# A gate's block ahead of the step from 32 to 64, and the bonus' sum behind the values

## The chip, the core and the metric

The kernel runs on one core of one Trainium2 chip. Five engines have instruction queues of their own: TensorE (PE, with its weight loads as PEld), VectorE (DVE), ScalarE (ACT), GpSimd (POOL) and SyncE (SP), which here only issues DMAs. The metric is the device time of one execution in microseconds (us).

## The reference: what is computed

One layer of a streaming encoder on 2048 tokens of width 1024, in float32:

```
h   = rms_norm(x)
P   = h @ w_in            # q,k,v of attention | r,k,v,w,a,g of the RWKV-7 branch | gates
yA  = chunk_band_attention(q, k, v)
yB  = rwkv7_time_mix(...)
m   = sigmoid(gA) * (yA @ proj_a) + sigmoid(gB) * (yB @ proj_b)
x   = x + rms_norm(m @ w_out)
x   = x + rms_norm(relu(rms_norm(x) @ w_up)^2 @ w_down)
```

The RWKV branch is, per head of 64 channels, a recurrence over time:

```
sa    = state @ aa_t
state = state * w_t + sa (x) bb_t + v_t (x) k_t
y_t   = state @ r_t
bonus = sum(r_t * k_t * r_k) * v_t
out   = (group_norm(y) + bonus) * g
```

The kernel computes it in chunks of 64 tokens. Within a chunk the recurrence becomes the inverse of a 64x64 unit triangular matrix, and between the chunks only a 64x64 state is carried.

## The kernel before

**Groups.** The first half works on four groups of 512 tokens: for each, `phase_rwkv`, then `phase_attention`, then `phase_merge`. The feed-forward layer follows (`phase_up`, `phase_down`); the change does not touch it.

**Dense blocks.** `dense(col)` multiplies 128 columns of `w_in` with the group's normed activations. Float32 is made of two rounded parts, so a block is 3 x 8 = 24 products of 128x128 by 128x512 (line 75). Its weights are loaded by SyncE (line 60), rounded by ScalarE (`whi`, line 66) and their low half is made by VectorE (`wlo`, line 67); there are two buffers of each, and two result banks (`psd`). The last product is kept as `self.mm`. A gate (`gate(i)`, line 657) is one such block, with a tanh on ScalarE (line 661) and a write to DRAM from ScalarE's queue; a group has 16 of them, and they are needed only in the merge, so that they can stand anywhere in the phase. `mix` (line 284) is such a block with the token shift behind it.

**One RWKV phase.** Eight heads are four pairs of heads, in two batches of two pairs. For each pair `rwkv_pre` makes r, k and v, the decays, the bonus and the chunks' matrices. For a batch `rwkv_inverse` inverts the two diagonal 32x32 blocks of every triangular matrix, with a chain of 31 steps of two instructions each on VectorE (lines 503 and 509), and turns the result into `X1` (line 512). `rwkv_blocks` then takes the step from 32 to 64: 64 small products of `NA` and `X1` on PE (line 533), a copy to `Z` on ScalarE (line 535), 64 small products of `Z` and `XT` (line 540), and a copy into `XT`. `rwkv_trans` makes the chunks' transitions, `recurrence` runs over the eight chunks (lines 613 to 616), and `rwkv_post` normalises the output (`yn`, line 634), transposes it (line 641), adds the bonus and multiplies with `g` (lines 651, 654).

**What sets the order.** The program is traced in one order, in which the generators `rec_of` and `rwkv_inverse` are advanced by hand between other work: `GATES` says how many gates the first `rwkv_pre` draws at its eight `between()` places, `STEPS` how many steps of the first batch's `rec_of` are traced at the places of the second batch's two `rwkv_pre`. Gates are drawn from one iterator, and once its 16 are gone a call of `gate()` does nothing. A planner in the compiler then fills each engine's queue: of the instructions that it reckons ready it takes the one traced first, so that later work can stand ahead of work traced before it which it holds for not ready yet. Once planned, an engine runs its queue in order and waits where an operand is not there.

In the first batch the step is traced at the first `between()` of the third pair, behind its r, k and v blocks. In the second batch it is traced behind the inverse, the first batch's post and one gate:

```
            rec = rec_of(NA, nxt, 1)
            for n in (4, 6, None):
                advance(rec, n)
                gate()
            gate(2)
            post = [self.rwkv_post(2 + q, nxt[q]) for q in range(2)]
```

In `rwkv_pre` the bonus' sum (a product of r*k*r_k with a block of ones, `ps_bonus`, line 426) stands ahead of the centred values' products (`ps_v`, line 435). Both take their banks from a pool with two buffers (`self.pa`), as do the transposes behind them (`ps_bk`, line 450).

Of the kernel before, what the change touches and what calls it, by code (L numbers as in the profile page):

```python
# [8 lines left out]
F32 = mybir.dt.float32  # L9
# [3 lines left out]
ALU = mybir.AluOpType  # L13
# [4 lines left out]
P = 128  # L18
# [5 lines left out]
G = 512  # L24
GT = G // P
C = 64
NC = G // C
# [10 lines left out]
RW0 = 1536  # L38
GATE0 = 1536 + 1792


def advance(steps, n=None):

    while n is None or n > 0:
        if next(steps, steps) is steps:
            return
        n = n and n - 1


class Block:  # L50
    def __init__(self, tc, a, out):
# [284 lines left out]
    def rwkv_pre(self, g, p, rp, NA, between=lambda: None):  # L336
        nc = self.nc
# [3 lines left out]
        r = self.tmp("r")  # L341
# [3 lines left out]
        ps = self.lora(0, p)  # L345
# [5 lines left out]
        ps = self.lora(1, p)  # L351
        ta = self.tmp("ta")
        nc.scalar.activation(ta, ps, AF.Tanh, scale=0.5, bias=self.ha0[:, col])
        v = self.tmp("v")
# [67 lines left out]
        between()  # L422

        nc.vector.scalar_tensor_tensor(r, r, self.rk[:, col], tk, op0=ALU.mult, op1=ALU.mult)
        psb = self.pa.tile([P, G], F32, tag="a", name="ps_bonus")
        nc.tensor.matmul(psb, self.bones, r, start=True, stop=True)
        nc.vector.tensor_tensor(r, psb, v, ALU.mult)
        nc.gpsimd.dma_start(self.bvd[p], r)

        between()  # L430

        SV = rp.tile([P, NC, 2, C], F32, tag="SV", name="SV")
# [4 lines left out]
        for h in range(2):  # L437
            src = psv[h * C : h * C + C]
            nc.scalar.copy(SVv[C:P, h, :, 0], src[:, :, 0:C])
            nc.scalar.copy(SVv[0:C, h, :, 1], src[:, :, C:P])  # L440
        R["SV"] = SV

        between()

# [15 lines left out]
        q = p % 2  # L460
        mS = self.mS[:, None, :].to_broadcast((P, 4, C))
        for h in range(2):
# [3 lines left out]
            for j in range(4):  # L466
                c = h * 4 + j
# [53 lines left out]
            nc.scalar.copy(XT[par * C : par * C + 32, :, :, 0:32], XD[par * C : par * C + 32])  # L521
        self.X1, self.XT = X1, XT

    def rwkv_blocks(self, NA, Rs):

        nc, X1, XT = self.nc, self.X1, self.XT
        Z = self.ip.tile([P, 2, NC, 32], F32, tag="Z", name="Z")
        parts = [(slice(r, r + 32), slice(r + 32, r + C)) for r in (0, C)]
        ps = self.pa.tile([P, 2, NC, 32], F32, tag="a", name="ps_t1")
        for q in range(2):  # L530
            for c in range(NC):
                for lo, hi in parts:
                    nc.tensor.matmul(ps[hi, q, c], NA[lo, q, c, 32:64], X1[lo, q, c], start=True, stop=True)
        for lo, hi in parts:
            nc.scalar.copy(Z[hi], ps[hi])
        ps = self.pa.tile([P, 2, NC, 32], F32, tag="a", name="ps_t2")
        for q in range(2):
            for c in range(NC):
                for lo, hi in parts:
                    nc.tensor.matmul(ps[lo, q, c], Z[hi, q, c], XT[hi, q, c, 32:64], start=True, stop=True)  # L540
        for lo, hi in parts:
            nc.scalar.copy(XT[lo, :, :, 32:64], ps[lo])
        for q in range(2):
            Rs[q]["XT"] = XT[:, q]
# [112 lines left out]
    def gate(self, i):  # L657
        nc = self.nc
        ps = self.dense(GATE0 + i * P)
        t = self.sp.tile([P, G], F32, tag="gate", bufs=2, name="gate")  # L660
        nc.scalar.activation(t, ps, AF.Tanh, scale=0.5, bias=self.hgb[:, i : i + 1])
        nc.scalar.dma_start(self.gd[i // 2][:, i % 2], t)

    def phase_rwkv(self, g):
        tc = self.tc
        with ExitStack() as ctx:
            def pool(name, bufs, **kw):
                return ctx.enter_context(tc.tile_pool(name=name, bufs=bufs, reuse_waits="tile", **kw))

            rp = pool("rw", 3)  # L670
            self.tp = pool("rwt", 9)
            self.ip = pool("rwi", 1)
            self.xp = pool("rwx", 2)
            self.lp = pool("rwl", 1)
            self.sp = pool("rws", 2)
            self.pa = pool("rwpa", 2, space=PSUM)
            self.pr = pool("rwpr", 2, space=PSUM)
            self.py = pool("rwpy", 2, space=PSUM)

            def pairs():  # L680
                return self.ip.tile([P, 2, NC, C], F32, tag="NA", name="NA")

            gates = iter(range(2 * KB))

            def gate(n=1):
                for i in range(n):
                    i = next(gates, None)
                    if i is not None:
                        self.gate(i)

            def places(plan, act):
                it = iter(plan)
                return lambda: act(next(it, 0))

            def rec_of(NA, Rs, b):
                self.rwkv_blocks(NA, Rs)
                yield
                for q in range(2):
                    yield from self.rwkv_trans(2 * b + q, Rs[q])
                    yield  # L700
                yield from self.recurrence(b, Rs)

            self.lora_wa(g)
            NA = pairs()
            between = places(GATES, gate)
            Rs = [self.rwkv_pre(g, q, rp, NA, between) for q in range(2)]
            inv = self.rwkv_inverse(NA, rp)
            for _ in range(2):
                advance(inv, 8)
                gate()  # L710
            advance(inv, 6)
            self.lora_g(g)
            advance(inv)
            gate()
            rec = rec_of(NA, Rs, 0)
            NA = pairs()
            between = places(STEPS, lambda n: advance(rec, n))
            nxt = [self.rwkv_pre(g, 2 + q, rp, NA, between) for q in range(2)]
            inv = self.rwkv_inverse(NA, rp)
            for n in (1, 4):  # L720
                advance(rec, n)
                gate()
            advance(rec)
            post = [self.rwkv_post(q, Rs[q]) for q in range(2)]
            for p in post:
                advance(p, 1)
            for _ in range(3):
                advance(inv, 8)
                gate()
            advance(inv)  # L730
            for p in post:
                advance(p)
# [7 lines that stand above are left out]
            for p in post:  # L740
                advance(p, 1)
            gate(2 * KB)
            for p in post:
                advance(p)
# [505 lines left out]
            self.phase_up(1, zp, rp, cb, pn, 8)  # L1250
            self.phase_down(1, zp, rp, cb, pn, lambda op, pt: iter(()))


_INS = [
    "x", "pre_mix_g", "w_in", "gate_bias", "rel_rev", "shift_mu", "w0", "w2", "a0", "a2", "g2",
    "k_k", "k_a", "r_k", "ln_x_w", "ln_x_b", "proj_a", "proj_b", "w_out", "post_mix_g",
    "pre_ffn_g", "w_up", "w_down", "post_ffn_g",
]


def layout(inputs):
    import numpy as np
# [7 lines left out]
            v = v.reshape(-1)  # L1270
        got[name] = np.ascontiguousarray(v)
    return got


# [15 lines left out]
```

## Time and profile before

| | |
|---|---|
| median of 3 runs | 3447.2 us (3445.45 to 3448.03) |
| profiled execution | 3443.36 us, its span 3441.7 us |
| mean granted clock of TensorE | 0.984 |
| TensorE, idle ahead of `ps_t` (line 533) | 26.6 us, 8 times |
| TensorE, idle ahead of `ps_bonus` (line 426) | 8.1 us, 8 times |

A row of the order of time gives the start and the duration in us, the engine, the line, the operation, what it writes and reads, the shape and the count; in brackets stands how long the engine was idle before it and what ended that. A row of the list of waits gives who waited for whom, the total in us, the number of times and the longest. A row of the table by stretches gives the stretch, its length, each engine's busy time with its count, the granted clock of TensorE (1 is full speed), the DMA share and GB/s. Times count from the start of the span. Products overlap in the array, so a product that lasts 0.39 us can start 0.23 us behind the one before it.

### The profile page before, as it was taken

What the parts mean: (1) busy time and instruction counts of PE and PEld (TensorE: products, weight loads), DVE (VectorE), ACT (ScalarE), POOL (GpSimd) and SP (SyncE); (2) the same over time, 40 slices, a digit from 0 to 9 for tenths busy, and PEclk for the clock granted to TensorE, in tenths of its full rate; (3) what the DMA queues carried; (4) which work ended last, traced back from release to release, by engine and by line L of the source; (5) the groups of instructions that cost most, each with busy time, mean ns of one, the idle gap of its engine ahead of it and who ended that gap; (6) DMA issues with size and microseconds to landing.
All of it is one profiled execution on the core that took longest, in us unless ns stands there. A gap on an engine that the chain in (4) does not pass through costs nothing. (4 is left out here: it accounts for less than half of the span.)

```text
span 3441.7 us, 50336 instructions
## 1 busy us (share of the span) xinstructions
PE 3301.4 (96%) x19233; PEld 2679.8 (78%) x19233; DVE 2414.4 (70%) x4110; ACT 1414.3 (41%) x2319; POOL 411.9 (12%) x796
## 2 busy tenths in 40 slices
PE   7999999999998999998999989999999999999998
PEld 5777777777876777876777877888888878888886
DVE  5774856766856775866774875777887788776667
ACT  4434634436644445644435634333331243331112
POOL 2210002111003110002210000111200021100001
PEclk9999999999999999999999999999999999999999
DMA  5223353125365225355224277434855374343233
GB/s 147 83 87 125 130 200 104 56 87 192 120 218 162 65 93 167 128 204 179 77 87 141 90 243 239 135 117 137 285 169 184 99 241 133 119 144 98 98 98 110
DMA packets 397864, 481.10 MB, mean 140 GB/s; under 512 B 17516, under 2 KB 304432, under 8 KB 397624
## 3 DMA queue, kind: packets, MB, share of 16 engines
q1 hardware_dynamic: 346168, 364.63, 33.2%
q0 software_dynamic: 23040, 79.71, 6.1%
q10 hardware_dynamic: 28416, 33.56, 2.8%
q8 instruction: 151, 2.47, 0.3%
q14 instruction: 89, 0.73, 0.1%
HBM read 356.16 MB, written 124.81 MB: 140 GB/s over the span
## 5 line engine op out<-in xcount | busy, mean ns | idle before, releaser
L75 PE MATMUL ps_dn<-fop 128*128 128x512 f32 x3072 | 700.9, 390 | 3.5 <-DVE u L1170 3.4
L75 PEld LDWEIGHTS ps_dn<-fop 128*128 128x128 f32 x3072 | 575.7, 188 | 125.1 <-DVE u L1170 5.2
L75 PE MATMUL psd<-hh,whi 128*128 128x512 f32 x1344 | 546.4, 407 | 9.7 <-ACT whi L66 8.8
L75 PE MATMUL psd<-hl,whi 128*128 128x512 f32 x1344 | 544.4, 405 | 0.0
L75 PE MATMUL psd<-hh,wlo 128*128 128x512 f32 x1344 | 541.2, 403 | 0.6 <-DVE wlo L67 0.5
L66 ACT CAST whi<-wraw 128x1024 fp32r<-128x1024 f32 x232 | 243.4, 1050 | 514.0 <-PE psd L75 411.1
L1170 DVE TENSOR_TENSOR u<-u,ps_dn 128x512 f32<-128x512 f32 x480 | 323.1, 685 | 148.5 <-PE ps_dn L75 148.0
L67 DVE TENSOR_TENSOR wlo<-wraw,whi 128x1024 fp32r<-128x1024 f32 x232 | 283.0, 1220 | 201.3 <-ACT whi L66 183.2
L75 PEld LDWEIGHTS psd<-hh,whi 128*128 128x128 f32 x1344 | 258.9, 193 | 63.3 <-ACT whi L66 10.0
L75 PEld LDWEIGHTS psd<-hh,wlo 128*128 128x128 f32 x1344 | 258.3, 192 | 51.7 <-DVE wlo L67 2.8
L75 PEld LDWEIGHTS psd<-hl,whi 128*128 128x128 f32 x1344 | 258.6, 192 | 50.3
L66 ACT CAST fop<-wdraw 128x1024 fp32r<-128x1024 f32 x64 | 67.0, 1047 | 424.0 <-DVE u L1170 321.2
L1091 POOL DMA_DIRECT2D ad<-r x128 | 69.5, 543 | 587.0 <-DVE r L1090 570.9
L75 PE MATMUL ps_p<-yh,whi 128*128 128x512 f32 x256 | 102.9, 402 | 10.7 <-DVE th L931 8.6
L66 ACT CAST s12h<-s 128x1024 fp32r<-128x1024 f32 x32 | 33.8, 1055 | 184.6 <-PE ps_u L75 184.6
L823 DVE CUSTOM_DVE_ANT_0 sc<-bias,ps_s 128x640 f32<-128x640 f32 (+4 forms) x128 | 93.5, 730 | 22.1 <-PE ps_pt L835 17.9
L960 PE MATMUL ps_o<-whi,mh 128*128 128x512 f32 x256 | 102.1, 403 | 5.1 <-ACT whi L66 3.5
L828 ACT ACTIVATE sc<-sc,mn 128x640 f32<-128x640 f32 (+4 forms) x128 | 97.7, 763 | 19.3 <-DVE mn L823 18.7
L839 ACT CAST PTh<-ps_pt 128x640 fp32r<-128x640 f32 (+4 forms) x128 | 80.0, 625 | 58.6 <-PE ps_pt L835 56.6
L75 PE MATMUL ps_p<-yh,wlo 128*128 128x512 f32 x256 | 103.0, 403 | 0.1
L75 PE MATMUL ps_p<-yl,whi 128*128 128x512 f32 x256 | 102.9, 402 | 0.0
L840 DVE TENSOR_TENSOR PTl<-ps_pt,PTh 128x640 fp32r<-128x640 f32 (+4 forms) x128 | 94.3, 737 | 12.1 <-ACT PTh L839 11.1
(352 smaller groups left out, 6648.8 us busy)
## 6 DMA issues: line engine op xcount, KB each, us to landing
wraw<-in_w_in_dram SPq DMA_DIRECT2D x168, 512.0 KB
wraw<-in_w_up_dram SPq DMA_DIRECT2D x80, 512.0 KB
ad<-r POOLq DMA_DIRECT2D x128, 256.0 KB, 2.6
wdraw<-in_w_down_dram SPq DMA_DIRECT2D x64, 512.0 KB
araw<-ad SPq DMA_DIRECT2D x64, 512.0 KB
gd<-gate ACTq DMA_DIRECT2D x64, 256.0 KB
th<-gd SPq DMA_DIRECT2D x32, 512.0 KB
wraw<-in_w_out_dram SPq DMA_DIRECT2D x32, 512.0 KB
```

What stands on the lines that cost most here:

```text
L66: self.nc.scalar.copy(hi, src)
L67: self.nc.vector.tensor_tensor(lo, src, hi.bitcast(F32), ALU.subtract)
L75: mm = nc.tensor.matmul(ps, l, r, start=n == 0, stop=n == last).ins
L823: nc.vector.tensor_tensor_reduce(sc[:, 0:n], bias[:, s0:640], pss[:, c0 : c0 + n], 1.0, 3.0e38, ALU.add, ALU.min, mn,)
L828: nc.scalar.activation(sc[:, 0:n], sc[:, 0:n], AF.Exp, scale=-1.0, bias=mn, accum_out=sm)
L839: nc.scalar.copy(hv, pst[:, 0:nk])
L840: nc.vector.tensor_tensor(lv, pst[:, 0:nk], hv.bitcast(F32), ALU.subtract)
L960: nc.tensor.matmul(ps[t], l[:, k, ts], r[:, k % 2], start=k == 0 and j == 0, stop=k == KB - 1 and j == 2)
L1091: nc.gpsimd.dma_start(self.ad[fb][:, th], r)
L1170: nc.vector.tensor_tensor(u[t][:, ns], u[t][:, ns], ps, ALU.add)
```

## The change

Two things. First, `rec_of` draws a gate ahead of the step, in both batches, and the first half of the step (the 64 products of line 533 and the copy to `Z`) is queued on TensorE behind the last product of that gate's block: `issue_after` adds an order on that engine's queue, not a wait. `rwkv_blocks` is cut in two for that, and `Z` is kept in `self.Z`. The planner may no longer place these products between earlier blocks or in the middle of the gate. As a group has 16 gates, the two drawn at the phase's end (`gate(2)`) are gone by then. Second, the bonus' sum, its product with v and its write to DRAM are traced behind the values' products and copies.

```diff
@@ rwkv_pre
         nc.vector.scalar_tensor_tensor(r, r, self.rk[:, col], tk, op0=ALU.mult, op1=ALU.mult)
-        psb = self.pa.tile([P, G], F32, tag="a", name="ps_bonus")
-        nc.tensor.matmul(psb, self.bones, r, start=True, stop=True)
-        nc.vector.tensor_tensor(r, psb, v, ALU.mult)
-        nc.gpsimd.dma_start(self.bvd[p], r)
-
         between()
 
         SV = rp.tile([P, NC, 2, C], F32, tag="SV", name="SV")
...
         R["SV"] = SV
+
+        psb = self.pa.tile([P, G], F32, tag="a", name="ps_bonus")
+        nc.tensor.matmul(psb, self.bones, r, start=True, stop=True)
+        nc.vector.tensor_tensor(r, psb, v, ALU.mult)
+        nc.gpsimd.dma_start(self.bvd[p], r)
 
         between()
@@ rwkv_blocks
-    def rwkv_blocks(self, NA, Rs):
+    def rwkv_blocks(self, NA, Rs, step):
 
         nc, X1, XT = self.nc, self.X1, self.XT
-        Z = self.ip.tile([P, 2, NC, 32], F32, tag="Z", name="Z")
         parts = [(slice(r, r + 32), slice(r + 32, r + C)) for r in (0, C)]
-        ps = self.pa.tile([P, 2, NC, 32], F32, tag="a", name="ps_t1")
...
-        for lo, hi in parts:
-            nc.scalar.copy(Z[hi], ps[hi])
+        if step == 0:
+            ps = self.pa.tile([P, 2, NC, 32], F32, tag="a", name="ps_t1")
+            for q in range(2):
+                for c in range(NC):
+                    for lo, hi in parts:
+                        nc.tensor.matmul(ps[hi, q, c], NA[lo, q, c, 32:64], X1[lo, q, c], start=True, stop=True)
+            self.Z = self.ip.tile([P, 2, NC, 32], F32, tag="Z", name="Z")
+            for lo, hi in parts:
+                nc.scalar.copy(self.Z[hi], ps[hi])
+            return
+        Z = self.Z
@@ phase_rwkv
             def rec_of(NA, Rs, b):
-                self.rwkv_blocks(NA, Rs)
+                gate()
+                with tc.issue_after(self.mm):
+                    self.rwkv_blocks(NA, Rs, 0)
+                self.rwkv_blocks(NA, Rs, 1)
                 yield
```

More of the change, by code (lines that the diff above doesn't have):

```diff
@@ L522, in rwkv_inverse @@
         self.X1, self.XT = X1, XT
-    def rwkv_blocks(self, NA, Rs):
+    def rwkv_blocks(self, NA, Rs, step):
         nc, X1, XT = self.nc, self.X1, self.XT
-        Z = self.ip.tile([P, 2, NC, 32], F32, tag="Z", name="Z")
         parts = [(slice(r, r + 32), slice(r + 32, r + C)) for r in (0, C)]
-        ps = self.pa.tile([P, 2, NC, 32], F32, tag="a", name="ps_t1")
-        for q in range(2):
-            for c in range(NC):
-                for lo, hi in parts:
-                    nc.tensor.matmul(ps[hi, q, c], NA[lo, q, c, 32:64], X1[lo, q, c], start=True, stop=True)
-        for lo, hi in parts:
-            nc.scalar.copy(Z[hi], ps[hi])
+        if step == 0:
[9 more added lines that the diff above has]
+        Z = self.Z
         ps = self.pa.tile([P, 2, NC, 32], F32, tag="a", name="ps_t2")
```

## The prediction

> **What bounds the kernel now.** I read the page's totals first, then TensorE's list of waits, then the order of time around the longest of them.
>
> ```profile
> span 3441.7 us, 50336 instructions
> PE 3301.4 (96%) x19233; PEld 2679.8 (78%) x19233; DVE 2414.4 (70%) x4110; ACT 1414.3 (41%) x2319; POOL 411.9 (12%) x796
> ```
>
> TensorE (PE) is busy for 96% of the span and the next engine for 70%. So PE's work, which the change leaves the same in amount, sets the time, and what can be won is PE's idle time (3441.7 - 3301.4 = 140 us) and products that run slowly. Both have an address. The list of waits, narrowed to PE, gives the wait, its total in us, how often it occurs and the longest:
>
> ```profile
> PE ps_t L533 <- DVE X L512: 26.6, 8, 3.8
> PE ps_ht L996 <- DVE xn L991: 24.7, 5, 7.4
> PE ps_bonus L426 <- DVE r L424: 8.1, 8, 1.2
> PE ps_bk L450 <- ACT SV L440: 0.9, 4, 0.2
> ```
>
> The first row is the step that the change moves (PE waits for the 32-blocks' inverse from VectorE), the third is the bonus' sum. The second belongs to the residuals, which the change leaves alone. The eight waits of the first row are two in each of the four groups. In order of time, on PE, the first of them (first batch):
>
> ```profile
> 146.70 0.39 PE L75 MATMUL psd<-hh,wlo 128*128 128x512 f32 x1
> 146.92 0.39 PE L75 MATMUL psd<-hh,whi 128*128 128x512 f32 x1
> 150.14 1.92 PE L533 MATMUL ps_t<-X,NA 32*32 32x32 f32 x64 [2.82 <-DVE X L512]
> 151.98 0.80 PE L75 MATMUL psd<-hl,whi 128*128 128x512 f32 x1
> 152.57 0.63 PE L75 MATMUL psd<-hh,wlo 128*128 128x512 f32 x1
> 153.00 0.63 PE L75 MATMUL psd<-hh,whi 128*128 128x512 f32 x1
> ```
>
> Two things are to be seen. PE stops in the middle of a block of 24 products although the next products stand right behind the 64 small ones. And after the wait the same 128x512 product starts every 0.43 us (152.57 to 153.00), where before it started every 0.225 us (146.70 to 146.92). The granted clock tells why. The table by stretches, for this kind of product alone, between the step's first and second round of small products at all eight places (two of them and the sum) and in one undisturbed stretch, and then the first round's small products (one place and the sum of all eight). Behind the stretch and its length stands PE's busy time in us with its count; the third number from the end is the granted clock:
>
> ```profile
> 151.98:157.17 5.19, 5.19 (x12) 3.80 (x12) 0.00 (x0) 1.27 (x2) 0.53 0.00 0
> 255.84:259.67 3.83, 3.83 (x9) 2.80 (x9) 0.00 (x0) 0.00 (x0) 0.55 0.46 137
> sum 36.41, PE 36.18 PEld 25.97 DVE 0.00 ACT 4.56; mean PE 4.52 PEld 3.25 DVE 0.00 ACT 0.57
> 295.03:309.20 14.17, 14.17 (x62) 11.56 (x62) 0.00 (x0) 1.36 (x2) 1.00 0.53 173
> 1163.20:1167.30 4.10, 1.20 (x64) 1.09 (x64) 0.99 0.42 124
> sum 41.35, PE 13.53 PEld 12.50; mean PE 1.69 PEld 1.56
> ```
>
> After each wait the clock is about half. Undisturbed, a product takes 14.17 / 62 = 0.228 us. The eight stretches hold 4 x 12 + 4 x 9 = 84 products in 36.18 us; at full clock they take 84 x 0.228 = 19.2, so 17.0 us are lost. The 64 small products take 13.53 us in all; where the clock was full they took 1.20, so 13.53 - 8 x 1.20 = 3.9 us are lost. The eight waits cost 26.6 + 17.0 + 3.9 = 47.5 us of PE time.
>
> The Trainium skill (TensorE: Matmul & The Clock Gate, HAM oscillation) says that the clock falls to half after idle gaps of over about 3.4 us. By that rule the four waits of 2.82 us would leave the clock alone and the loss would be some 11 us smaller. The trace disagrees (0.53 behind a wait of 2.82 us), and the measurement decides.
>
> **The change part by part.** *The gate ahead of the step.* No block is added: a gate is 24 products, 24 x 0.228 = 5.5 us, and two of a group's 16 are drawn earlier, so that the two which the phase draws last (5.5 us each) find nothing left. What each place gets depends on what PE did there before. First batch: how much of the interrupted block (the next pair's r) was done?
>
> ```profile
> 155.85 0.59 ACT L289 COPY pr<-psd 128x512 f32<-128x512 f32 x1 [1.29 <-PE psd L75]
> 149.03 1.05 DVE L512 STREAM_TRANSPOSE X<-X 128x512 f32<-128x512 f32 x1
> ```
>
> Its result is read at 155.85, so it ends with the eighth product after the wait (151.98 + 0.59 + 6 x 0.43 + 0.63 = 155.8): 16 were done, 8 were left. The gate, earlier in program order than that block, takes its place. PE then does 8 more products, 8 x 0.228 = 1.8 us, ahead of the step and still waits 2.8 - 1.8 = 1.0 us for the inverse, which VectorE ends at 150.08. Is 1.0 us short enough to keep the clock? The nearest wait is the bonus' of 1.23 us at 105.08, and the stretch around it has 1.00:
>
> ```profile
> 105.00:112.00 7.00, 6.70 (x42) 5.25 (x43) 4.60 (x9) 1.47 (x4) 0.59 (x1) 1.00 0.35 112
> ```
>
> Second batch:
>
> ```profile
> 249.76 0.39 PE L75 MATMUL psd<-hh,wlo 128*128 128x512 f32 x1
> 253.99 1.92 PE L533 MATMUL ps_t<-X,NA 32*32 32x32 f32 x64 [3.83 <-DVE X L512]
> 255.84:265.80 9.96, 6.47 (x18) 4.39 (x18) 0.00 (x0) 0.00 (x0) 0.83 0.18 54
> 265.62 1.05 ACT L66 CAST whi<-wraw 128x1024 fp32r<-128x1024 f32 x1 [0.30 <-PE psd L75]
> 244.09 1.22 DVE L67 TENSOR_TENSOR wlo<-wraw,whi 128x1024 fp32r<-128x1024 f32 x1
> 252.87 1.06 DVE L512 STREAM_TRANSPOSE X<-X 128x512 f32<-128x512 f32 x1
> 253.82 1.19 DVE L67 TENSOR_TENSOR wlo<-wraw,whi 128x1024 fp32r<-128x1024 f32 x1
> ```
>
> Here the block that PE left is itself a gate, and ScalarE gets its buffer at 265.62, after 18 more products: 6 were done, 18 are left. The step now stands behind all of them: 18 x 0.228 = 4.1 us against a wait of 3.83, so the wait goes and the step starts about 0.3 us later than now. Its weights are there: the low half that it reads was made at 244.09, between the inverse's steps; the one at 253.82 is the next block's.
>
> So of 47.5 us, 4 x 1.0 = 4.0 stay and 43.5 go. Bounds: all 47.5, if the first batch's inverse ends 1 us earlier; 43.5 - 4.0 = 39.5, if another 1 us stays in each batch-one wait.
>
> What else the gate issues moves with it and stays the same in number: one weight load on SyncE's queue, the two halves on ScalarE (1.05) and VectorE (1.22), the tanh on ScalarE and its write from ScalarE's queue. Two weight buffers exist, so at any point of PE's order as many halves lie ahead of the inverse as now; nothing is added to VectorE's chain. If one did slip in, the inverse would end 1.22 us later; in the first batch that would show in full, 4 x 1.2 = 5 us. The result tile that is now kept between the two parts costs nothing: the same copies write it.
>
> *The end of the phase, which loses two gates.* The rows, ScalarE's tanh of the last gates, VectorE's normalised outputs of both last pairs, PE's transposes of them, and the start of attention:
>
> ```profile
> 298.30 0.69 DVE L634 TENSOR_TENSOR yn<-ps_y,grs 128x512 f32<-128x512 f32 x1 [2.07 <-POOL grs L632]
> 299.28 0.68 ACT L661 ACTIVATE gate<-psd,hgb 128x512 f32<-128x512 f32 x1
> 301.63 0.69 DVE L634 TENSOR_TENSOR yn<-ps_y,grs 128x512 f32<-128x512 f32 x1 [2.05 <-POOL grs L632]
> 309.23 1.03 PE L641 MATMUL ps_yt<-ident,yn 128*64 128x128 f32 x8
> 310.15 0.68 ACT L661 ACTIVATE gate<-psd,hgb 128x512 f32<-128x512 f32 x1
> 317.43 0.69 DVE L654 TENSOR_TENSOR yf<-yf,ps_g 128x512 f32<-128x512 f32 x1
> 318.78 0.59 ACT L772 ACTIVATE QA<-psd 64x512 fp32r<-64x512 f32 x1
> 324.25 0.47 PE L75 MATMUL psd<-hh,whi 128*128 128x512 f32 x1 [0.79 <-DVE QA L775]
> ```
>
> Today gates fill PE from the recurrence's end to 309.23 (the stretch from 295.03 above, busy throughout), and the outputs, ready at 299.0 and 302.3, wait for PE. Without two gates PE comes 10.9 us earlier, at 298.3: 0.7 us before the first output and, after the transposes (1.0) and the products behind them (1.5), up to 1.5 us before the second: at most 2.2 us a group. Attention's first blocks, 5.5 us each, need neither and can fill this. Only the third must wait for the first one's results to be read, as it does today (0.79). I take 1.0 us a group, 4 in all; ends 0 and 2.2 x 4 = 9.
>
> *The bonus' sum behind the values.*
>
> ```profile
> 105.08 1.12 PE L426 MATMUL ps_bonus<-r,bones 128*128 128x512 f32 x2 [1.23 <-DVE r L424]
> 106.04 1.05 PE L435 MATMUL ps_v<-cmat,v 128*128 128x128 f32 x8
> 106.85 0.48 PE L75 MATMUL psd<-hl,whi 128*128 128x512 f32 x1
> 107.13 0.37 ACT L439 COPY SV<-ps_v 64x256 f32<-64x256 f32 x1 [4.28 <-PE ps_v L435]
> ```
>
> The values' products (1.05 us) need only v. Placed in the wait they would hide 1.05 of 1.23 us and all of the other 0.80, 4 x 1.85 = 7.4 us. But dense products follow at 106.85, so PE had work to put there already; what made it wait is where the sum was placed in the queue, and the values may simply push dense products back. That row is nearer to no gain: I take 2 us. The other end: the transposes behind now get the buffer that the four copies (0.37 each) leave; today they wait 0.9 us in all, and as the copies' 1.5 us stand against the sum's 1.12, 16 times 0.4 would be 6 us lost, were no dense product at hand. The bonus' write moves back about 1 us on GpSimd's queue, and its reader, in the second half of the post, comes two stages later.
>
> **Sum.** -43.5 - 2 + 4 = -41.5 us. The profiled execution took 3443.4 us (span 3441.7), 3.8 under the median of 3447.2; its waits are taken as those of the median: 3447.2 - 41.5 = 3405.7.
>
> **The rivals.**
> *The end of the phase takes much of it.* If attention's blocks don't fill the end, PE idles 2.2 us for the outputs and, at a guess, half of the 5.5 us from 318.78 to 324.25 for the reading of its first results; so long a wait brings the half clock, (17.0 + 3.9) / 8 = 2.6 us. 4 x 7.5 = 30 us instead of 4: 3447.2 - 45.5 + 30 = about 3432. Against it: attention's products already stand among the post's.
> *Slower: the gate has no weights when its turn comes.* If VectorE's low half stands behind the inverse, as the one at 253.82 does, PE stops at the gate's third product, idles until 255.0 instead of 253.99, and then runs 22 products before the step, which comes 1.0 + 22 x 0.228 = 6 us later. The waits stay and grow by 8 x 1.0; the 6 us show only in the second batches, which have few gates behind them, and I take half, 4 x 3: 3447.2 + 8 + 12 = 3467, and 3479 in full. Such a place loses some 4 us and a spared one gains 47.5 / 8 = 5.9, so it decides from five of the eight places on. Against it: the half at 244.09. The Trainium skill (the same page, Part 2) says that matmuls stay in program order, so that a stopped gate would stop the step too. The trace agrees: from 146.92 on the dense products behind the step stood still with it.
> *It doesn't do what it says.* The gate is done earlier, in place of other blocks, and the step again comes where the inverse isn't ready: 3447. Against it: before 146.92 PE has no gap into which a gate could go.
>
> **Numbers.** Forecast 0.68 (its own range 3391 to 3421: best -47.5 - 7.4 - 0 = -55, worst -39.5 + 9 + 5 = -26); end of the phase 0.12; no change 0.05; slower 0.15. From 3391 to 3440 the range leaves 0.20 outside. 0.2% (7 us) is about what a measurement of this kernel tells from no change. Faster 0.80, same 0.05, slower 0.15.
>
> **What would show it.** Right: the waits of the step fall from 26.6 to about 4 us, the half clock vanishes behind them, two tanh rows stand ahead of the steps and none between the last recurrence and the transposes. Wrong: a wait of psd for wlo ahead of the step, or waits of ps_yt for yn, or of attention's first products, of over 2 us a group.

## The result and the profile after

The change takes 3461.3 us (median of 6 runs, 3452.5 to 3463.9) where the kernel before takes 3447.6 in the same session: a ratio of 1.0036, 95% interval 1.0026 to 1.0046. It is 0.36% slower, and the prediction said 1.2% faster. The profiled execution took 3463.3 us.

From the page of the change, the busy time of each engine:

```profile
span 3461.6 us, 50334 instructions
PE 3305.0 (95%) x19233; PEld 2682.7 (77%) x19233; DVE 2413.5 (70%) x4110; ACT 1414.2 (41%) x2319; POOL 402.5 (12%) x796
```

And from its list of waits, narrowed to TensorE, the rows that answer to those of before:

```profile
PE ps_t L541 <- ACT Z L534: 20.9, 8, 3.7
PE ps_vt L792 <- ACT vf L789: 8.5, 6, 2.5
PE ps_bonus L437 <- DVE r L422: 6.8, 8, 1.4
PE ps_g L73 <- DVE yn L635: 6.0, 4, 1.5
PE psd L73 <- ACT v L290: 3.2, 4, 0.8
PE ps_yt L642 <- DVE yn L635: 2.5, 4, 0.6
PE ps_t L531 <- DVE X L510: 0.8, 3, 0.4
```

The last row is the wait that the change was about: 26.6 us have become 0.8, where the prediction left 4.0. The first row is new. The second round of the step's small products (line 541; line 540 before) now waits for `Z`, which ScalarE copies from the first round's result, in the same eight places, and for 20.9 us. The wait has moved from one half of the step to the other. Three more rows are new: `ps_g` and `ps_yt` wait at the phase's end for the normalised outputs, 8.5 us together, and dense products (`psd`) wait for `v` in the first batches, 3.2 us.

The place shows best in the second batch of the first group. TensorE's order of time:

```profile
257.39 0.39 PE L73 MATMUL psd<-hh,wlo 128*128 128x512 f32 x1
257.85 1.20 PE L531 MATMUL ps_t<-X,NA 32*32 32x32 f32 x64
258.98 0.50 PE L73 MATMUL psd<-hh,whi 128*128 128x512 f32 x1
...
260.24 0.40 PE L73 MATMUL psd<-hh,wlo 128*128 128x512 f32 x1
264.30 0.31 PE L541 MATMUL ps_t<-XT,Z 32*32 32x32 f32 x2 [3.66 <-ACT Z L534]
264.54 0.80 PE L73 MATMUL psd<-hh,whi 128*128 128x512 f32 x1
265.13 0.63 PE L73 MATMUL psd<-hl,whi 128*128 128x512 f32 x1
265.56 0.63 PE L73 MATMUL psd<-hh,wlo 128*128 128x512 f32 x1
```

The first round starts without a wait. Six dense products follow, and then TensorE stands for 3.66 us. Before, nine dense products stood between the two rounds of a second batch and twelve in a first one, and they covered the making of `Z`. The gate ahead of the step has taken such products to the other side of the first round; six and five are left behind it. The full clock shortens this cover once more: the nine lasted 3.8 us at half clock, the six last 1.7 (258.98 to 260.64).

What `Z` waits for is in ScalarE's order of time, and what that waits for is in VectorE's:

```profile
259.48 1.25 ACT L517 COPY XT<-XD 32x512 f32<-32x512 f32 x2 [5.70 <-DVE XD L512]
260.75 1.24 ACT L519 COPY XT<-XD 32x512 f32<-32x512 f32 x2
262.01 1.04 ACT L64 CAST whi<-wraw 128x1024 fp32r<-128x1024 f32 x1
262.96 0.68 ACT L662 ACTIVATE gate<-psd,hgb 128x512 f32<-128x512 f32 x1
263.67 0.58 ACT L534 COPY Z<-ps_t 32x512 f32<-32x512 f32 x1
```

```profile
256.62 1.17 DVE L510 STREAM_TRANSPOSE X<-X 128x512 f32<-128x512 f32 x1
257.65 1.20 DVE L65 TENSOR_TENSOR wlo<-wraw,whi 128x1024 fp32r<-128x1024 f32 x1
258.77 0.68 DVE L512 STREAM_TRANSPOSE XD<-X 128x512 f32<-128x512 f32 x1
```

The first round ends at 257.85 + 1.20 = 259.05, but `Z` is copied at 263.67. Ahead of it stand the inverse's four copies to `XT` (2.5 us), the next block's weights (1.04) and the gate's own tanh (0.68). The copies could not start before 259.48, because `XD` stands behind a `wlo` of 1.20 us on VectorE. The Trainium skill (TensorE: Matmul & The Clock Gate, Part 1) says that ScalarE takes its instructions strictly in order; the trace agrees, with a copy that is 4.6 us late behind six instructions that it does not need, while ScalarE stood idle until 259.48. (The second round itself also reads what the two copies of line 517 write.) In the kernel before, `wlo` stood ahead of `XD` at this place too (253.82 and 254.92), but ScalarE's queue had the copies to `Z` first:

```profile
255.95 1.17 ACT L535 COPY Z<-ps_t 32x512 f32<-32x512 f32 x2 [5.71 <-PE ps_t L533]
257.14 1.26 ACT L519 COPY XT<-XD 32x512 f32<-32x512 f32 x2
```

The third cost is the clock. Stretches of 3.41 us around this place, and the two at the first batch's step; behind the stretch stands TensorE's busy time, and the third number from the end is the granted clock:

```profile
259.71:263.12 3.41, 0.93 (x4) 0.40 (x3) 0.03 (x1) 3.35 (x6) 0.00 (x0) 1.00 0.56 159
263.12:266.53 3.41, 2.23 (x7) 1.78 (x8) 1.19 (x1) 1.68 (x3) 0.00 (x0) 0.50 0.49 146
...
269.95:273.36 3.41, 3.41 (x20) 2.59 (x20) 0.00 (x0) 1.69 (x5) 0.00 (x0) 0.50 0.00 0
273.36:276.77 3.41, 3.41 (x60) 2.90 (x58) 0.00 (x0) 1.29 (x4) 0.00 (x0) 1.00 0.02 5
...
150.49:153.90 3.41, 1.43 (x6) 0.86 (x6) 1.95 (x3) 3.36 (x7) 0.18 (x1) 1.00 0.40 115
153.90:157.31 3.41, 3.41 (x35) 2.40 (x37) 3.38 (x7) 2.11 (x3) 0.00 (x0) 0.50 0.20 77
```

The clock is half from 263.12 to 273.36, for 10.2 us. In the first batch no single wait is long (0.78 for `v`, 1.58 for `Z`), and the clock falls all the same.

Where the time went, by phases. For the four groups together, the sum rows of the table by stretches, first of RWKV and then of attention and merge, of the kernel before and of the change:

```profile
sum 1195.54, PE 1106.57 PEld 882.50 DVE 760.60 ACT 505.35 POOL 225.11; mean PE 276.64 PEld 220.63 DVE 190.15 ACT 126.34 POOL 56.28
sum 905.50, PE 877.93 PEld 710.76 DVE 644.13 ACT 502.75 POOL 60.04; mean PE 219.48 PEld 177.69 DVE 161.03 ACT 125.69 POOL 15.01
```

```profile
sum 1202.28, PE 1106.80 PEld 882.64 DVE 763.07 ACT 505.54 POOL 218.34; mean PE 276.70 PEld 220.66 DVE 190.77 ACT 126.39 POOL 54.59
sum 917.51, PE 879.95 PEld 712.40 DVE 640.94 ACT 502.65 POOL 58.73; mean PE 219.99 PEld 178.10 DVE 160.24 ACT 125.66 POOL 14.68
```

TensorE's products are the same in both, so its busy time (PE) measures the clock, and the sum less PE its idle time. In RWKV the idle time rose from 89.0 to 95.5 us and the busy time is 1106.6 and 1106.8: of what the slow products had cost, nothing was won. Attention and merge are 12.0 us longer, though their queues are the same. How much of that belongs to the change is taken up with the last experiments.

### The profile page after: what moved, and what is told of

It reads as the page before. It is cut to its first block, busy times and chain, and to the rows that moved or that the text cites. A ratio compares the mean times of both kernels' runs of the same rounds, so it can differ in the third digit from the quotient of the medians.

```text
span 3461.6 us, 50334 instructions
## 1 busy us (share of the span) xinstructions
PE 3305.0 (95%) x19233; PEld 2682.7 (77%) x19233; DVE 2413.5 (70%) x4110; ACT 1414.2 (41%) x2319; POOL 402.5 (12%) x796
## 5 line engine op out<-in xcount | busy, mean ns | idle before, releaser
L964 PE MATMUL ps_o<-wlo,mh 128*128 128x512 f32 x256 | 101.5, 396 | 1.9 <-DVE wlo L65 1.9
```

The lines of the kernel that those rows point to most:

```text
L964: nc.tensor.matmul(ps[t], l[:, k, ts], r[:, k % 2], start=k == 0 and j == 0, stop=k == KB - 1 and j == 2)
```

## The experiments

**Theory:** the wait for X1 is gone, and the wait for `Z` behind ScalarE's queue, with the half clock that it brings, has taken its place. **Rivals:** the phase's end, which lost two gates, is the price; the queue rule is; the bonus' new place is.

### The gates alone

```diff
             def rec_of(NA, Rs, b):
+                gate()
                 self.rwkv_blocks(NA, Rs)
```

> Edit: the kernel before, with one gate drawn ahead of the step in both batches and nothing else: no queue rule, the step not cut in two, the bonus where it was. Theory (the wait is only moved: the step's second products now wait for the copy to Z on ScalarE, and the half clock with them): +10 to +18 us against before, as in the whole change; idle ahead of the second products (XT, Z) 15 to 21 us, ahead of the first under 2 us. Rival 1 (the bonus' move costs the time): within 3 us of before, or faster. Rival 2 (the queue rule costs it): the first products wait for the inverse again, over 15 us, and the time is within 5 us of before.

Measured: 3441.5 us, 0.9972 of the kernel before (0.9961 to 0.9982). The gates gain 0.28% where a loss was expected. Of this kernel the list of waits, VectorE's order of time in the first group's second batch, and the table by stretches there:

```profile
PE ps_t L540 <- ACT Z L535: 14.7, 8, 2.3
PE ps_t L533 <- DVE X L512: 4.0, 4, 1.0
```

```profile
255.57 0.71 DVE L514 STREAM_TRANSPOSE XD<-X 128x512 f32<-128x512 f32 x1
256.20 1.18 DVE L67 TENSOR_TENSOR wlo<-wraw,whi 128x1024 fp32r<-128x1024 f32 x1
```

```profile
257.38:260.79 3.41, 1.80 (x20) 1.15 (x14) 0.88 (x2) 3.34 (x6) 0.00 (x0) 1.00 0.72 209
260.79:264.21 3.42, 3.09 (x72) 2.45 (x73) 0.35 (x1) 0.94 (x3) 0.00 (x0) 1.00 0.71 204
```

The first products' wait is the forecast 4 x 1.0 us. The wait for `Z` is there too, but at most 2.3 us long: here `XD` stands ahead of `wlo`, so ScalarE's copies start sooner. In the first of the two stretches TensorE idles 1.6 us, and the clock stays full. Over the four RWKV phases TensorE's busy time falls to 1088.5 us, 18 less than before, while its idle time stays at 90.0. So within RWKV the gates' gain is the clock's alone; the idle time has moved.

### The bonus alone

```diff
-        psb = self.pa.tile([P, G], F32, tag="a", name="ps_bonus")
         ...
         R["SV"] = SV
+        psb = self.pa.tile([P, G], F32, tag="a", name="ps_bonus")
```

(with its three following lines)

> Edit: the kernel before, with the bonus' sum behind the values, and no gate moved. Theory (the gates carry the loss): -5 to +4 us against before. Rival 1 (the bonus' move costs the time): +10 to +16 us. Its idle time ahead of the bonus' sum: 8.1 us before, 6.8 with the whole change; theory 5 to 8.

Measured: 3447.6 us, 0.9988 (0.9978 to 0.9998): some 4 us less. The bonus' wait falls from 8.1 to 6.8 us, while the wait for X1 grows from 26.6 to 29.0. So each part of the change, alone, makes the kernel a little faster, by 0.28% and 0.12%; together they make it 0.36% slower. Next to the gates alone, the kernel that has both has `wlo` ahead of `XD` in the second batches, and in the first ones the read of `v` behind the four copies (the 0.78 us above): the bonus' move shifts the inverse and the blocks against each other. Why the planner orders them so was not tried.

### The gate ahead of the step in one batch only

```diff
+                if b == 0:
+                    gate()
                 self.rwkv_blocks(NA, Rs)
```

> Edit: the kernel before, with a gate drawn ahead of the step in the first batch alone; one gate is left for the phase's end. Theory (moved wait, batch by batch): the first batches' wait goes from the first products to the second (4 x 1.6 us), those of the second batches stay at 4 x 3.8; +3 to +9 us. Rival 3 (the phase's end, which lacks two gates, is the whole cost): one gate of 5.5 us is left there and covers the 2 us by which PE comes too early, so within 3 us of before or faster.

> Edit: the kernel before, with a gate drawn ahead of the step in the second batch alone; one gate is left for the phase's end. Theory (moved wait): the second batches' 4 x 3.8 us ahead of the first products go and 4 x 3.7 come ahead of the second; the recurrence behind ends 5 to 10 us later; +4 to +10 us. Rival 3 (the phase's end alone): within 3 us of before or faster.

 (with `b == 1`)

Measured: the first batch alone 3439.9 us, 0.9975 (0.9962 to 0.9987); the second alone 3461.9 us, 1.0030 (1.0018 to 1.0042). The list of waits of the second:

```profile
PE ps_t L540 <- ACT Z L535: 14.4, 4, 3.6
PE ps_t L533 <- DVE X L512: 11.3, 4, 2.8
```

Four waits for `Z` of 3.6 us in the second batches, with `wlo` ahead of `XD` as in the change, and the loss is nearly the whole change's. In the first batches a gate ahead leaves waits for `Z` of 1.6 us at most, and gains where a loss was expected. Yet with gates in both batches nothing is lost (0.9972, above): there `XD` stands ahead of `wlo` in the second batches, and the wait is at most 2.3 us. So the second batch is where the change loses, and not the place alone decides but also the order that the planner makes there.

### `Z` copied by VectorE

```diff
-                nc.scalar.copy(self.Z[hi], ps[hi])
+                nc.vector.tensor_copy(self.Z[hi], ps[hi])
```

> Edit: the whole change, with the copies to Z (between the step's two rounds of products) on VectorE in place of ScalarE, where they stand behind the inverse's four copies, the next block's rounding and the gate's tanh. Theory (the second round waits for Z behind ScalarE's queue, 3.66 us in the second batches, and this halves the clock for 10 us): the wait ahead of the second round falls from 20.9 us to under 8, the half clock behind the step goes, and the time falls by 12 to 25 us, to 3436 to 3450. Rival 3 (the phase's end without its two gates is the cost): still 8 to 15 us above before, whatever the wait.

> Edit: the gates drawn ahead of the step in both batches, without the queue rule and with the bonus where it was (as in the first experiment), and the copies to Z on VectorE. Theory: the remaining wait of 14.7 us ahead of the second round falls to under 8, so 3 to 10 us faster than the first experiment, 12 to 20 us faster than before. Rival 3: no faster than the first experiment.

 (in the kernel with the gates alone)

Measured: in the change 3441.2 us, 0.9972 (0.9962 to 0.9982); with the gates alone 3428.8 us, 0.9946 (0.9928 to 0.9963). From the list of waits of the first:

```profile
PE ps_t L541 <- DVE Z L534: 6.5, 4, 1.6
PE ps_at L558 <- ACT XT L543: 4.9, 4, 1.2
```

Taking `Z` out of ScalarE's queue, and nothing else, gives 20 us back (3461.3 to 3441.2), as expected: the wait falls from 20.9 to 6.5 us, and 4.9 us appear behind the next copy in that queue. With the gates alone the wait ahead of the second round falls from 14.7 to 4.8 us, and the kernel gains 13 us (3441.5 to 3428.8).

### The copies to `XT` on GpSimd

```diff
-            nc.scalar.copy(XT[r0 + 32 : r0 + 64, :, :, 32:64], XD[r0 + 32 : r0 + 64])
+            nc.gpsimd.tensor_copy(XT[r0 + 32 : r0 + 64, :, :, 32:64], XD[r0 + 32 : r0 + 64])
...
-            nc.scalar.copy(XT[par * C : par * C + 32, :, :, 0:32], XD[par * C : par * C + 32])
+            nc.gpsimd.tensor_copy(XT[par * C : par * C + 32, :, :, 0:32], XD[par * C : par * C + 32])
```

In the change:

> Edit: the whole change, with the inverse's four copies into XT on GpSimd in place of ScalarE; the copy to Z stays on ScalarE. Theory: Z is made some 2.5 us earlier (four copies of 0.62), so that the wait in the second batches falls from 3.7 us to about 1 to 2, unless GpSimd's copies become the last; 8 to 20 us faster than the change. Rival 3 (the phase's end): as the change, +8 to +15 us against before.

In the kernel before, in the one with the gates alone, and in the one with the gate in the first batch only:

> The kernel before with the inverse's four copies of XT on GpSimd, and nothing of the change. If the copies in ScalarE's queue are what takes the change's gain away (theory), they cost the kernel before less: its first products wait for X1 (26.6 us) and not for Z, so this wait stays at 20 us or more, with its half clock, and the time is within 10 us of before (3440 to 3452). If the copies themselves are the cost in either order of the work (rival), this kernel gains as much as the change did from the same edit, 40 us, and comes to 3410.

> The kernel before with all gates ahead of the step and the copies of XT on GpSimd; the bonus stays before the values. Theory: neither product of the step waits more than 2.3 us, no half clock behind it, RWKV near 1160 us over the four groups, the time 3412 to 3428, as the change with the same copies (0.9910 of before). If the bonus after the values is worth its predicted 2 us there, this one is 2 us longer than that; if the bonus' place costs (rival: the first inverse comes earlier, the read of v later), it is 3 to 8 us shorter.

> The gate ahead of the step in the first batch alone, and the copies of XT on GpSimd: one gate is left for the end of the phase. Theory with the phase's end at 2 us a group: against all gates ahead, 8 us are won at the ends and later, but the second batch's first products wait for X1 again (11 us with a half clock of some 7 us a group): 3420 to 3435, slower than all gates ahead. Rival: the end of the phase and attention behind it are the larger price (12 us over four groups): 3405 to 3415, faster than all gates ahead.

| kernel | copies on ScalarE | copies on GpSimd |
|---|---|---|
| before | 1 | 1.0041 (1.0026 to 1.0056), 3463.0 us |
| gate ahead, first batch | 0.9975 | 0.9966 (0.9954 to 0.9979), 3438.3 us |
| gates ahead, both | 0.9972 | 0.9935 (0.9920 to 0.9949), 3426.5 us |
| the change | 1.0036 | 0.9910 (0.9895 to 0.9925), 3419.8 us |

The same edit costs 0.4% without the gates and gives 1.3% with the change; with the gate in the first batch only, the intervals overlap. In the change it gives 41 us (3461.3 to 3419.8), twice the 8 to 20 that were expected. So the copies are no cost in themselves; they are one where the second round stands close behind the first. Waits and RWKV's sum row of the change with copies on GpSimd:

```profile
PE ps_t L541 <- POOL XT L517: 1.8, 4, 0.5
PE ps_t L531 <- DVE X L510: 0.4, 2, 0.2
```

```profile
sum 1158.69, PE 1082.85 PEld 863.13 DVE 768.20 ACT 485.15 POOL 252.88; mean PE 270.71 PEld 215.78 DVE 192.05 ACT 121.29 POOL 63.22
```

Both rounds now run almost without waiting, and RWKV takes 36.9 us less than before: 13.1 of idle time (89.0 to 75.8) and 23.7 of busy time. This kernel is faster than the change and than the kernel before. Without the gates the edit leaves the first wait as it was, and TensorE's busy time rises (the same two views):

```profile
PE ps_t L533 <- DVE X L512: 26.8, 8, 4.0
```

```profile
sum 1201.28, PE 1113.18 PEld 888.15 DVE 766.89 ACT 485.67 POOL 247.15; mean PE 278.29 PEld 222.04 DVE 191.72 ACT 121.42 POOL 61.79
```

That it would be slower by so much was not expected. The half-clock stretches that begin behind the eight steps last 65 us in its trace, against 48, 31 and 37 in the three profiles of the kernel before; between its two rounds only four dense products are left. Whether the one brings the other was not tried. The gate in the first batch only, which keeps one gate for the phase's end, is 12 us slower than both gates ahead: what is won at the step outweighs what the end loses. And the bonus' place, with gates and free copies, seems to be worth 0.9935 - 0.9910 = 0.25%, some 8 us, though the two intervals overlap a little.

### The phase's end without its gates

```diff
             for n in (1, 4):
                 advance(rec, n)
-                gate()
+                gate(2)
```

> Edit: the kernel before, with two more gates drawn behind the second pairs' preparation (two in place of one at both places of that loop), so that, as in the change, none is left for the phase's end; no gate directly ahead of the step's trace, the bonus where it was. Theory (the loss is the wait behind the step): TensorE has 11 us more work beside the second inverse and comes to the step after it, so that the second round waits under 2.5 us and keeps the clock: 2 to 12 us faster than before. Rival 3 (the phase's end): the outputs are waited for, 2 us a group, and attention begins behind: 5 to 15 us slower than before.

Measured: 3474.0 us, 1.0066 (1.0051 to 1.0081), where the theory expected a gain and its rival a loss of 15 us at most. The two gates were to leave the end alone, but at their new place they push back more than themselves:

```profile
PE ps_yt L641 <- ACT yf L646: 16.2, 4, 4.1
PE ps_t L533 <- DVE X L512: 11.3, 4, 2.8
...
PE ps_g L75 <- DVE yn L634: 6.0, 4, 1.5
...
PE ps_yt L641 <- DVE yn L634: 2.5, 4, 0.6
```

The first row is the first batch's post, which now waits ahead of the second step. So this run does not measure the end by itself. What it and the change share are the last two rows, 8.5 us or 2.1 us a group, in a kernel with no gate drawn for the step itself. All eight profiled kernels with no gate left for the end have these two rows (6.0, and 2.5 to 2.8), and none of the eight profiles with one or both left has either: that much is the end's, in TensorE's waits.

### The queue rule, and the scatter

```diff
-                with tc.issue_after(self.mm):
-                    self.rwkv_blocks(NA, Rs, 0)
+                self.rwkv_blocks(NA, Rs, 0)
```

> The change without the rule that queues TensorE's products of the step behind the gate's block. The instruction queues of all five engines are the same as the change's, so the time is the change's, 0.2 to 0.5% above the kernel before, with a wait for Z of 20 to 22 us. If the rule did anything on the chip, the time would leave that range. As a second profile of the same queues it gives attention and merge again: 915 to 920 us if the change makes them longer, 905 to 912 if that is scatter.

The kernel before, unchanged, twice more:

> The kernel before, unchanged, profiled a second time. In its first profile attention and merge took 905.5 us over the four groups and the four RWKV phases 1195.5. If the longer attention and merge of the change (917.5) is the work of the change, this profile shows 903 to 908 again. If it is scatter between executions, this profile lies between 908 and 920, and only the RWKV phases' difference is the change's.

> The kernel before, unchanged, profiled a third time, to see how much attention and merge scatter: within 3 us of the first two profiles if they are steady, 5 us and more off if not. The RWKV phases, whose waits are set by the order of the work, stay within 3 us of 1195.5.

Measured: without the rule 3461.9 us, 1.0031 (1.0020 to 1.0042), with a wait for `Z` of 21.0 us. All five engines have the same queues with and without the rule: the planner puts the step behind the gate anyway. The rule costs and gives nothing, and the run is a second profile of the change.

| us, four groups | span | RWKV | its idle | its busy | attention and merge |
|---|---|---|---|---|---|
| before | 3441.7 | 1195.5 | 89.0 | 1106.6 | 905.5 |
| before, second | 3447.6 | 1193.4 | 90.8 | 1102.6 | 912.3 |
| before, third | 3450.6 | 1196.7 | 93.4 | 1103.3 | 911.0 |
| change | 3461.6 | 1202.3 | 95.5 | 1106.8 | 917.5 |
| change, second | 3462.2 | 1195.6 | 95.4 | 1100.2 | 920.7 |

The profile of before that the prediction used was short in attention and merge by some 6 us. On the means, the change costs 15.3 us: 3.7 in RWKV (+4.4 idle, -0.7 busy), 9.5 in attention and merge, 2 in the rest. Over all profiles, attention and merge go with the gates left for the phase's end: 905.5 to 920.3, mean 912.1, with both left (five profiles); 913.9 to 919.5, mean 916.5, with one (three); 914.5 to 921.8, mean 919.2, with none (eight). The 920.3 is the kernel before with copies on GpSimd, which changes nothing there. So some 7 us appear to follow the missing gates, but the groups overlap, and the cause within attention stays open. The row that grows most is `ps_vt` waiting for `vf`, from 3.7 to 8.5 us. In the last three groups `vf` stands in ScalarE's queue behind the rounding of `vr`, which is read back from DRAM, and ScalarE's waits for `vr` come to 8.5 to 11.1 us in the three profiles of before and to 14.3 and 16.0 in the two of the change. So the late operand appears to be a transfer; no run tests it.

## Why the prediction was wrong

**The step.** "So of 47.5 us, 4.0 stay and 43.5 go" is the step that failed. Its premises held: PE is the bound, the first products' wait goes (4 x 1.0 us left with the gates alone, to the digit; 0.8 in the change, where the bonus' move lets the first inverse end at 146.85 us in place of 150.08), and a wait of that size halves the clock. The conclusion left out what is late next. The 43.5 were 22.6 us of idle time and 20.9 of slow products. The waits of the step's two halves together fell by 26.6 - 0.8 - 20.9 = 4.9 us, and the busy time by 0.7 on the means. The size of the term is about right for a kernel in which `Z` hardly waits: the change with copies on GpSimd saves 26.6 - 0.4 - 1.8 = 24.4 us of these waits and 23.7 of busy time in RWKV, 48 us, of which other waits, the end's above all, take 11 back. (The slow products were read from one profile; in the other two of the kernel before RWKV's busy time is 3.3 and 4.0 us lower.)

**"What else the gate issues moves with it ... nothing is added to VectorE's chain."** The count was right and the conclusion wrong. The weights' rounding and the tanh stand on ScalarE ahead of `Z`, behind four copies that the prediction never named; and `wlo` stood ahead of `XD`, which feeds those copies, in the second batches, as it did before the change, when `Z` was copied first. The dense products between the rounds, which the prediction used only to measure the clock, were the cover for `Z`; the gate took half of them (21 in a group's two batches became 11), and the full clock that was hoped for shortens the rest.

**The end of the phase** was taken at 4 us with 9 as the upper end. In TensorE's waits it is 8.5, close to that end, and up to some 9 us more lie in attention and merge, of which 7 appear to be its own. That 9 comes so close is partly luck: by the prediction's own rows, 2.5 us of work from 299.0 leave 0.8 before 302.3, not 1.5, so that 1.5 and not 2.2 was its bound for a group. Measured are 0.6 and 1.5, because less work stood between.

**The bonus** was taken at -2 us; alone it measured -4 (0.02% to 0.22%), its wait fell by 1.3. What was missed is that it shifts the order of VectorE and ScalarE around the step: added to the gates with copies on ScalarE it costs 1.0036 - 0.9972 = 0.64%, with copies on GpSimd it seems to give 0.25%. (The cut of the step in two, which comes with it in both, was not tried alone.)

**The sum again**, by measured terms (waits from the first profile of each, the rest from the means): waits of the step -4.9, slow products -0.7, bonus -1.3, the end's waits +8.5, the new wait for `v` +3.2, attention and merge +9.5: +14.3, against 15.3 between the mean spans. The range had two slips of its own: -55 gives 3392 and not 3391, and the worst end leaves out the 6 us that the bonus could lose. Neither would have reached 3461.

**The rivals.** The slower one (the gate without weights, 3467) has the right sign but the wrong mechanism: no wait for `wlo` stands ahead of the step; `wlo` cost time as the obstacle ahead of `XD`. Its test, waits of psd for `wlo`, would not have found it. The end of the phase is a part, not the whole. "It doesn't do what it says" is wrong: the change does just that.

## What to carry to other kernels

When a wait on a chain is to be removed by moving work ahead of it, follow the same chain to its next wait and ask what covers that one now: often it is the very work that is moved. List, on each engine that the chain passes through, the instructions that stand ahead of the chain's own, in queue order, before counting a gain. An edit's worth depends on its neighbours here: the same four copies moved to another engine cost 0.4% before the change and gave 1.3% after it.

## What the runs showed of the clock

The half clock comes in whole stretches. In the change's trace the sixteen stretches begin on one grid of 3.413 us, within 0.03 us over the whole span, and last 1, 2, 3 or 5 steps of it (the last is cut off by the span's end). In the second profile of the same queues the grid lies elsewhere, and the same wait in the second group's second batch (3.65 us there, 3.64 in the first profile) brings 3.4 us at half clock (from 751.1) instead of 10.2 (from 754.6). That may be part of why executions of one kernel differ by some microseconds.

All sixteen profiles were cut into windows of their grids (from about 35 to 3400 us), and TensorE's idle time was taken in each. Of 15319 windows at full clock, 228 were followed by half clock, and these had 1.51 us of idle time or more; the other 15091 had 1.92 or less. So the line lies between these, near half a window, and it is the idle time within a window that counts, not the longest wait: in the window from 150.49 above, the wait of 1.58 us and the last 0.40 of the wait for `v` were enough (1.43 busy of 3.41), while with the gates alone a wait of 1.94 us across a border (1.61 and 0.33) was not. The Trainium skill (TensorE: Matmul & The Clock Gate, Part 1) gives a free-running window of 3413 ns; the trace agrees. It names one idle window as the condition for the fall; the traces differ, as less than 2 us of idle time in a window were enough, and the measurement decides.
